# Decay sums of an SSD mixer read back from a DRAM scratch, and dt computed from the residual stream

## The chip, the cores and the metric

One core of a Trainium2 chip. Times are device microseconds (us) of one launch. The engines are named as in the profile: PE (matmuls) with PEld (its weight loads), DVE (VectorE), ACT (ScalarE), POOL (GpSimd), SP (which issues most DMAs).

## The reference, cut to what matters

Two layers (DEPTH 2), each a half-step SwiGLU FFN, a mixer and another half-step FFN, over 256 prompt tokens and 8 x 4 sample tokens (T = 288 columns), D_MODEL 1024. The part that is changed is the decay of the mixer's SSD branch, 16 heads, chunks of 128 tokens:

```
h  = rmsnorm(x, mix_norm)
dt = softplus((h @ w_in)[dt columns, 16] + dt_bias)
la = dt * (-exp(a_log))
acum = cumsum(la)                                  # per head, within a chunk
decay = exp(where(causal, acum[t] - acum[s], -inf))
y_diag = einsum(cb * decay, x * dt)                # cb = C.B per group
to_end = exp(acum[-1] - acum); from_start = exp(acum)
```

## The kernel before, in words

The activations lie transposed: feature on the partitions, 288 tokens along the free axis, `x` as 8 tiles of 128 features. Every large product runs in three float32r parts (`mm3`, line 271): weight high x activation high, high x low, low x high. The weights arrive as 439 slabs of 8 tiles of 128 x 128 (`Stream`): SP loads a slab (`raw`, 4 buffers), ACT makes the high part (`whi`, line 137, 4 buffers), DVE the low part (`wlo`, line 145, 3 buffers), PE runs 24 matmuls on it (`ps`). The high part is asked for three slabs ahead, the low part two.

The order of all work is written by hand. At the start of each slab `tick` loads, splits, and calls `step`, which runs every small generator of the mixer (`dt_work`, `conv`, `heads4`, ...) up to its next `yield`; a delay given to `W.start` counts such steps. Each engine executes what it was given in that order. Matmul results go to 7 rotating PSUM banks (tag `b`).

What the change touches:

- Lines 603 to 606 split the 1024 x 16 dt weights into a high and a low part side by side (`wds`, 48 columns); line 1242 on runs 16 float32r matmuls on them with the high and low part of the normed input (`ps_dt`).
- `dt_work` (line 663) forms dt and its cumulative sums `nac` (16 heads x 288) and splits them once more into `nst`. With masked copies (`sbd`) and products with ones (`ps_ee`, `ps_rb`, `ps_eb`) it spreads the sample group's sums over the partitions, into `Ee`, `Eb` and `Ms`.
- `heads4(g)` (line 859) handles four heads of the prompt group. `rows` multiplies `nst` with one broadcast column of `sel2`, so that a head's row of 256 sums stands on all 128 partitions in PSUM (`ps_row`); `decay` reads it from there into `E` on ACT; `E` is multiplied by the masked C.B on DVE and enters `outputs` on PE (`ps_y`). `E` has two buffers. The four calls start at steps 7, 11, 15 and 19 (line 1196).

Of the kernel before, what the change touches and what calls it, by code (L numbers as in the profile page):

```python
# [38 lines left out]
H = 16  # L39
# [146 lines left out]
def trunk_kernel(ctx, tc, wpack, xT, memT, vecs, consts, wdt, wpool, hpool, hconv, h0T, kT, vC,  # L186
# [46 lines left out]
    def tt(out, a, b, op, eng=None):  # L233
        (eng or V).tensor_tensor(out=out, in0=a, in1=b, op=op)  # L234
# [13 lines left out]
    def act(out, a, func, **kw):  # L248
        A.activation(out=out, in_=a, func=func, **kw)  # L249

    W = Stream(nc, rawp, splp, wpack)

    vec = cp.tile([P, V_TOT], F32, name="vec")
# [13 lines left out]
    def hi_of(hi, src, scale=None):  # L267
        if scale is None:
            act(hi, src, AF.Copy)
        else:  # L270
            act(hi, src, AF.Copy, scale=scale)

    def lo_of(lo, src, hi, scale=None):
        if scale is None:
            tt(lo, src, hi.bitcast(F32), ALU.subtract)
        else:
            stt(lo, src, scale, hi.bitcast(F32), ALU.mult, ALU.subtract)
# [172 lines left out]
    rv = cp.tile([P, 2], F32, name="rv")  # L450
    sel2 = cp.tile([P, H], F32R, name="sel2")
    nst = cp.tile([P, TP], F32R, name="nst")
    G.memset(nst.bitcast(F32), 0.0)
    sel4 = cp.tile([P, 4], F32R, name="sel4")
# [14 lines left out]
    def mem_norm():  # L469
        for c in range(KC):  # L470
            src = chunk(mem, c)[:, :NM]
            if c == 0:
                act(macc, src, AF.Square)
            else:
                sq = tmp("sqr", NM)
                act(sq, src, AF.Square)
                tt(macc, macc, sq, ALU.add)
            if c % 4 == 3:
                yield
        yield  # L480
        r = rstd_cols([macc], (0, P), D, "mem")
        V.tensor_copy(out=rv, in_=r)
        yield
        ps = bank("ps_rm")
        for j in range(2):
            mm(ps[:, j * P:(j + 1) * P], rv[:, j:j + 1].to_broadcast([P, P]), ident)
        act(Rm, ps[:, :NM], AF.Copy)
        act(sel4, ident.rearrange("p (a b) -> p a b", a=4)[:, :, 0], AF.Copy)
        act(sel2, con[:, K_SEL:K_SEL + H], AF.Copy)

# [106 lines left out]
    def mixer(i, cur, nxt):  # L597
# [4 lines left out]
        nc.sync.dma_start(out=wd, in_=wdt[i])  # L602
        wds = sp.tile([P, KC, 48], F32R, tag="wds", name="wds")
        G.memset(wds[:, :, H:2 * H].bitcast(F32), 0.0)
        hi_of(wds[:, :, 0:H], wd)
        lo_of(wds[:, :, 2 * H:], wd, wds[:, :, 0:H])
        wp_ = sp.tile([P, 4, P], F32, tag="wp", name="wp")
# [32 lines left out]

        npar = sp.tile([32 + H, T], F32, tag="nac", name="nac")
        nac, par = npar[:H], npar[32:, :P]
        nact = sp.tile([P, 3, H], F32, tag="nact", name="nact")
# [19 lines left out]
        def dt_work(ps_dt):  # L663
            dtr = tmp("dtr", T, 48)
            tt(dtr, ps_dt[:48, :T], cur.R[:48], ALU.mult)
            S = [P, 3, H]
# [5 lines left out]
            for j, (a, n) in enumerate(CH):  # L672
                mm(pt[:n, j * H:(j + 1) * H], dtr[:, a:a + n], con[:48, K_SEL:K_SEL + H])
            bias = vec[:, i * V_N + V_DT:i * V_N + V_DT + H]
# [31 lines left out]
            mm(pw[:TS, 2 * H:3 * H], sst, la[:TS, 2, :])  # L706
            act(nst[0:H, :], ph[:H, :TP], AF.Copy)
            V.tensor_copy(out=nac, in_=ph[:H, :T])
            tt(nst[32:32 + H, :], nac[:, :TP], nst[0:H, :].bitcast(F32), ALU.subtract)
            act(wt[:, 0, :], pw[:, 3 * H:4 * H], AF.Exp, scale=-1.0)  # L710
            act(wt[:, 1, :], pw[:, H:2 * H], AF.Exp, scale=-1.0)
            act(wt[:TS, 2, :], pw[:TS, 2 * H:3 * H], AF.Exp, scale=-1.0)
            ts(b01, pw[:, 0:H], -1.0, ALU.mult)
            ex = tmp("dex", TS, H)
            act(ex, nac[:, TP:T], AF.Exp, scale=-1.0)
            act(par, con[:H, K_PAR:K_PAR + P], AF.Copy)
            sb = wide("sbd", P, TP)
            hh = H // 2
            for j in range(2):
                o = sb[96 * j:96 * j + H, :]  # L720
                tt(o.rearrange("p (h t) -> p h t", h=hh), nac[:, TP:T].unsqueeze(1).to_broadcast([H, hh, TS]),
                   ident[:H, hh * j:hh * j + hh].unsqueeze(2).to_broadcast([H, hh, TS]), ALU.mult)
            tt(sb[32:32 + H, :].rearrange("p (a t) -> p a t", a=8), ex.unsqueeze(1).to_broadcast([H, 8, TS]),
               con[:H, K_PM:K_PM + 8].unsqueeze(2).to_broadcast([H, 8, TS]), ALU.mult)
            tt(sb[64:64 + H, :P].rearrange("p (b h) -> p b h", b=DB), seg(ex)[:, :, 3:4].to_broadcast([H, DB, H]),
               ident[:H, :H].unsqueeze(1).to_broadcast([H, DB, H]), ALU.mult)
            yield
            pt, pd = bank("ps_nact"), bank("ps_ee")
            for j, (a, n) in enumerate(CH):
                PE.transpose(pt[:n, j * H:(j + 1) * H], nac[:, a:a + n], ident[:H, :H])  # L730
            mm(pd[:, :P], ones[64:64 + H, :], sb[64:64 + H, :P])
            yield
            ts(nact[:, 0:2].rearrange("p a h -> p (a h)"), pt[:, :2 * H], -1.0, ALU.mult)
            V.tensor_copy(out=nact[:TS, 2], in_=pt[:TS, 2 * H:3 * H])
            V.tensor_copy(out=Ee.rearrange("p b h -> p (b h)"), in_=pd[:, :P])
            pr = [bank("ps_rb") for j in range(2)]
            pe = bank("ps_eb")
            mm(pr[0][:, :TP], ones[:H, :], sb[:H, :])
            mm(pe[:, :TP], par, sb[32:32 + H, :])
            mm(pr[1][:, :TP], ones[96:96 + H, :], sb[96:96 + H, :])  # L740
            yield
            V.tensor_copy(out=Eb.rearrange("p a t -> p (a t)"), in_=pe[:, :256])
            for j in range(2):
                tt(Ms[:, hh * j:hh * j + hh], nact[:TS, 2, hh * j:hh * j + hh].unsqueeze(2).to_broadcast([TS, hh, TS]),
                   pr[j][:TS, :TP].rearrange("p (h t) -> p h t", h=hh), ALU.subtract)
            ts(Ms, Ms, 0.0, ALU.min)
# [112 lines left out]
        def heads4(g):  # L859
# [3 lines left out]
            def rows(pi):  # L863
                prow = bank("ps_row")
                for j in range(2):
                    h = 4 * g + 2 * pi + j
                    mm(prow[:, j * TP:(j + 1) * TP], sel2[:, h:h + 1].to_broadcast([P, P]), nst)
                return prow

            def decay(pi, prow):  # L870

                E = ep.tile([P, 2, 3 * P], F32, tag="E", name="E")
                for j in range(2):
                    h = 4 * g + 2 * pi + j
                    for t_ in range(2):
                        act(E[:, j, TP * t_:TP * t_ + P], prow[:, j * TP + P * t_:j * TP + P * t_ + P], AF.Relu,
                            bias=nact[:, t_, h:h + 1])
                    act(E[:, j, P:TP], prow[:, j * TP + P:(j + 1) * TP], AF.Exp, scale=-1.0, bias=b01[:, h:h + 1])
                e = E.rearrange("p j (a t) -> p j a t", a=3)[:, :, 0:3:2, :]
                act(e, e, AF.Exp, scale=-1.0)  # L880
                return E

# [15 lines left out]
            def finish(pi, py):  # L898
# [5 lines left out]
                nc.sync.dma_start(out=o_ssm_p[i, p], in_=st)  # L904

            px = bank("ps_x")
            for t_ in range(2):
                for pi in range(2):
                    k = t_ * TP + pi * P
                    PE.transpose(px[:, k:k + P], chunk(xsu, 2 * g + pi)[:, t_ * P:(t_ + 1) * P], ident)  # L910
            r0 = rows(0)
            yield
# [5 lines left out]
               wt[:, 0:2, hs].unsqueeze(3).to_broadcast([P, 2, 4, 64]), ALU.mult)  # L918
            E0 = decay(0, r0)
            r1 = rows(1)  # L920
            yield
            E1 = decay(1, r1)
            yield
            for E in (E0, E1):
                tt(E, E, cbm[:, g, :].unsqueeze(1).to_broadcast([P, 2, 3 * P]), ALU.mult)
            yield
            ys = outputs((E0, E1))
            yield
# [254 lines left out]
        for kind, cs, tiles, cuts in mixer_groups():  # L1183
# [10 lines left out]
            if kind == "u" and c == 0:  # L1194
                items["xss"] = W.start(xss_work(), 3)
                items["pairs"] = [W.start(sample_diag(), 6)] + [W.start(heads4(g), 7 + 4 * g) for g in range(4)]
                items["ss"] = [W.start(sample_state(b), 14 + 2 * b) for b in range(DB)]
                items["yo"] = W.start(sample_y(), 33)
                items["gn"] = W.start(group_norm(), 36)
# [38 lines left out]
            elif kind == "q":  # L1238
# [4 lines left out]
                for k in range(KC):  # L1243
                    mm(ps_dt[:48, :T], wds[:, k, :], chunk(xh, k), k == 0, False)
                    mm(ps_dt[:48, :T], wds[:, k, :], chunk(xl, k), False, k == KC - 1)
                items["dt"] = W.start(dt_work(ps_dt))
# [137 lines left out]
```

## Time and profile before

| | us |
|---|---|
| median of 3 runs (lowest, highest) | 1548.44 (1547.94, 1549.15) |
| the profiled execution, whole | 1547.92 |
| its span, first to last instruction | 1546.1 |
| PE busy | 1530.3 |
| DVE busy | 1064.0 |
| ACT busy | 824.3 |
| POOL busy | 192.1 |

Busy times are unions of an engine's instructions within the span; a matmul's end is modelled, and matmuls overlap in the pipeline, so what one costs is the distance from its start to the next start, not its own duration. The engines overlap each other. One profiled execution was read; it lies 0.5 us below the median.

### The profile page before, as it was taken

The page shows a single profiled execution, that of the slowest core. Times are in us where ns is not written, and L with a number is a line of the kernel's source. Part 1 is how long each engine was busy: PE and PEld are TensorE (multiplying, and loading weights), DVE is VectorE, ACT ScalarE, POOL GpSimd, SP SyncE. Part 2 cuts the span into 40 slices and gives each one's busy share as a digit, 9 for nine tenths or more (in the row PEclk, how much of TensorE's full clock was granted, in tenths as well). Part 3 has the DMA queues.
Part 4 walks back from the last instruction along what each step waited for, and adds up shares of the span by engine and source line. Part 5 has one row for each costly group of instructions (what it writes and reads, how often), then busy time and mean ns, then how long its engine had stood idle before and what let it go on. Part 6 is the DMA issues. An engine that isn't in the chain of part 4 may idle for free.

```text
span 1546.1 us, 29133 instructions
## 1 busy us (share of the span) xinstructions
PE 1530.3 (99%) x11740; PEld 1491.3 (96%) x11740; DVE 1064.0 (69%) x1674; ACT 824.3 (53%) x1268; POOL 192.1 (12%) x284
## 2 busy tenths in 40 slices
PE   9999999999999999999999999999999999999998
PEld 7999999899989999999999999999998999999997
DVE  7766655899678877665566665579978787766643
ACT  7544444566864645444445444457587464544442
POOL 0100001245003111000010000024600120100001
PEclk9999999999999999999999999999999999999999
DMA  8655455566466445455545544556655745555552
GB/s 294 220 167 166 168 165 171 188 231 230 147 210 221 164 157 173 164 167 169 166 152 173 168 164 164 171 190 206 230 172 193 249 152 162 166 165 167 166 169 73
DMA packets 80711, 278.00 MB, mean 180 GB/s; under 512 B 9024, under 2 KB 13248, under 8 KB 80576
## 3 DMA queue, kind: packets, MB, share of 16 engines
q1 hardware_dynamic: 79872, 275.28, 53.5%
q8 instruction: 92, 1.51, 0.4%
q10 hardware_dynamic: 704, 0.86, 0.2%
q14 instruction: 43, 0.35, 0.1%
HBM read 262.39 MB, written 13.71 MB: 179 GB/s over the span
## 4 chain that ended last, share of the span: by engine, by line
PE 93%; DVE 4%; ACT 1%; issue 1%; DMA 1%; ACTq 0%; DVEq 0%
PE ps L246 65%; PE pd L246 18%; PE ps_v L246 1%; PE ps_y L246 1%; PE ps_k L246 1%; DVE wlo L145 1%; DVE cacc L243 1%; PE ps_up L246 1%; PE ps_yo L246 1%; PE ps_sp L246 0%; PE ps_pv L246 0%; ACT whi L137 0%; PE ps_cb L246 0%; DVE cbuf L234 0%; DMA cb<-kT 0%
## 5 line engine op out<-in xcount | busy, mean ns | idle before, releaser
L145 DVE TENSOR_TENSOR wlo<-raw,whi 128x1024 fp32r<-128x1024 f32 (+1 forms) x441 | 552.3, 1254 | 255.8 <-ACT hidh L249 102.5
L137 ACT ACTIVATE whi<-raw 128x1024 fp32r<-128x1024 f32 (+1 forms) x441 | 464.0, 1054 | 328.1 <-PE ps L246 161.1
L246 PE MATMUL ps<-n1h,whi 128*128 128x288 f32 x896 | 270.6, 302 | 4.1 <-DVE gate L234 2.1
L246 PE MATMUL ps<-n1l,whi 128*128 128x288 f32 x896 | 264.4, 295 | 0.0
L246 PE MATMUL ps<-n1h,wlo 128*128 128x288 f32 x896 | 263.7, 294 | 0.0
L246 PE MATMUL ps<-n2h,whi 128*128 128x288 f32 x704 | 208.9, 297 | 0.0
L246 PE MATMUL ps<-n0h,whi 128*128 128x288 f32 x704 | 208.8, 297 | 0.0
L246 PE MATMUL pd<-hidh,whi 128*128 128x288 f32 x704 | 208.4, 296 | 0.0
L246 PE MATMUL ps<-n0l,whi 128*128 128x288 f32 x704 | 207.8, 295 | 0.0
L246 PE MATMUL pd<-hidl,whi 128*128 128x288 f32 x704 | 207.8, 295 | 0.0
L246 PE MATMUL ps<-n2l,whi 128*128 128x288 f32 x704 | 207.8, 295 | 0.0
L246 PE MATMUL ps<-n0h,wlo 128*128 128x288 f32 x704 | 207.1, 294 | 0.0
L246 PE MATMUL pd<-hidh,wlo 128*128 128x288 f32 x704 | 207.1, 294 | 0.0
L246 PE MATMUL ps<-n2h,wlo 128*128 128x288 f32 x704 | 207.1, 294 | 0.0
L246 PEld LDWEIGHTS ps<-n1h,whi 128*128 128x128 f32 x896 | 168.1, 188 | 8.5 <-DVE gate L234 2.5
L246 PEld LDWEIGHTS ps<-n1l,whi 128*128 128x128 f32 x896 | 168.4, 188 | 0.6
L246 PEld LDWEIGHTS ps<-n1h,wlo 128*128 128x128 f32 x896 | 168.6, 188 | 0.0
L234 POOL TENSOR_TENSOR acc<-acc,sqr 128x288 f32<-128x288 f32 x42 | 48.6, 1158 | 801.3 <-ACT sqr L249 800.0
L246 PEld LDWEIGHTS ps<-n2h,wlo 128*128 128x128 f32 x704 | 132.7, 188 | 0.0
L246 PEld LDWEIGHTS pd<-hidh,wlo 128*128 128x128 f32 x704 | 132.7, 188 | 0.0
L246 PEld LDWEIGHTS ps<-n0h,wlo 128*128 128x128 f32 x704 | 132.7, 188 | 0.0
L246 PEld LDWEIGHTS ps<-n0l,whi 128*128 128x128 f32 x704 | 132.2, 188 | 0.1
(314 smaller groups left out, 2720.2 us busy)
## 6 DMA issues: line engine op xcount, KB each, us to landing
raw<-wpack SPq DMA_DIRECT2D x439, 512.0 KB, 3.3
cb<-kT SPq DMA_DIRECT2D x16, 512.0 KB, 5.5
cb<-vC SPq DMA_DIRECT2D x16, 512.0 KB, 4.9
hb<-h0T SPq DMA_DIRECT2D x16, 512.0 KB, 5.5
o_ssm_s<-hb SPq DMA_DIRECT2D x16, 512.0 KB, 5.0
x<-xT SPq DMA_DIRECT2D x4, 288.0 KB, 6.1
o_mk<-ksb SPq DMA_DIRECT2D x2, 512.0 KB, 6.1
o_mv<-vsb SPq DMA_DIRECT2D x2, 512.0 KB, 5.4
```

What stands on the lines that cost most here:

```text
L137: nc.scalar.activation(out=hi[:, a], in_=self.loaded[self.n_hi][:, a], func=AF.Copy)
L145: nc.vector.tensor_tensor(out=lo[:, a], in0=raw[:, a], in1=self.his[n][:, a].bitcast(F32), op=ALU.subtract)
L234: (eng or V).tensor_tensor(out=out, in0=a, in1=b, op=op)
L243: V.scalar_tensor_tensor(out=out, in0=a, scalar=s, in1=b, op0=op0, op1=op1)
L246: PE.matmul(out, lhsT=lhsT, rhs=rhs, start=start, stop=stop)
```

## The change

dt comes from the unsplit residual `x` in plain float32: the norm's gain is multiplied into the 1024 x 16 weights, which stand in 32 columns (16 of them zero), and the eight products go to four column groups of the PE array in turn; their four partial sums are added by the transposing matmul with `sel4h`. The sums `nac` and the exponentials of the sample group are written to a DRAM scratch `sums`, the last ones of each sample to `lasts`; `Ms`, `Eb` and `Ee` are read back from there by SP with stride 0 over the partitions. `rows` becomes two DMAs issued by POOL that read a pair of heads' sums straight into `E`; the ACT instructions of `decay` work there in place. `heads4` has one more step, and its four calls start at steps 6, 11, 16 and 21.

```diff
+    sums = nc.dram_tensor("sums", (L, H, T + TS), F32).ap()
+    lasts = nc.dram_tensor("lasts", (L, DB, H), F32).ap()
...
-        wds = sp.tile([P, KC, 48], F32R, tag="wds", name="wds")
-        G.memset(wds[:, :, H:2 * H].bitcast(F32), 0.0)
-        hi_of(wds[:, :, 0:H], wd)
-        lo_of(wds[:, :, 2 * H:], wd, wds[:, :, 0:H])
+        wds = sp.tile([P, KC, 2 * H], F32, tag="wds", name="wds")
+        G.memset(wds[:, :, H:], 0.0)
+        gain = vec[:, i * V_N + V_MIX:i * V_N + V_MIX + KC]
+        tt(wds[:, :, 0:H], wd, gain.unsqueeze(2).to_broadcast([P, KC, H]), ALU.mult)
...
-            dtr = tmp("dtr", T, 48)
-            tt(dtr, ps_dt[:48, :T], cur.R[:48], ALU.mult)
+            dtr = tmp("dtr")
+            tt(dtr, ps_dt[:, :T], cur.R, ALU.mult)
...
-                mm(pt[:n, j * H:(j + 1) * H], dtr[:, a:a + n], con[:48, K_SEL:K_SEL + H])
+                mm(pt[:n, j * H:(j + 1) * H], dtr[:, a:a + n], sel4h)
...
-            act(nst[0:H, :], ph[:H, :TP], AF.Copy)
-            V.tensor_copy(out=nac, in_=ph[:H, :T])
-            tt(nst[32:32 + H, :], nac[:, :TP], nst[0:H, :].bitcast(F32), ALU.subtract)
+            V.tensor_copy(out=nac[:, :T], in_=ph[:H, :T])
+            ex = nac[:, T:]
+            act(ex, ph[:H, TP:T], AF.Exp, scale=-1.0)
...
-            for j in range(2):
-                o = sb[96 * j:96 * j + H, :]
-                tt(o.rearrange("p (h t) -> p h t", h=hh), nac[:, TP:T].unsqueeze(1).to_broadcast([H, hh, TS]),
-                   ident[:H, hh * j:hh * j + hh].unsqueeze(2).to_broadcast([H, hh, TS]), ALU.mult)
...
...
-            mm(pd[:, :P], ones[64:64 + H, :], sb[64:64 + H, :P])
+            nc.sync.dma_start(out=sums[i], in_=nac)
+            nc.sync.dma_start(out=lasts[i].rearrange("b h -> h b").unsqueeze(2), in_=seg(ex)[:, :, 3:4])
             yield
...
-            mm(pr[0][:, :TP], ones[:H, :], sb[:H, :])
-            mm(pe[:, :TP], par, sb[32:32 + H, :])
-            mm(pr[1][:, :TP], ones[96:96 + H, :], sb[96:96 + H, :])
-            yield
-            V.tensor_copy(out=Eb.rearrange("p a t -> p (a t)"), in_=pe[:, :256])
+            nc.sync.dma_start(out=Ms, in_=sums[i, :, TP:T].unsqueeze(0).to_broadcast([TS, H, TS]))
...
+                nc.sync.dma_start(out=Eb[64 * j:64 * j + 64], in_=src.to_broadcast([64, 8, TS]))
+            nc.sync.dma_start(out=Ee, in_=lasts[i].unsqueeze(0).to_broadcast([P, DB, H]))
+            yield
+            yield
+            tt(Ms, nact[:TS, 2].unsqueeze(2).to_broadcast([TS, H, TS]), Ms, ALU.subtract)
...
             def rows(pi):
-                prow = bank("ps_row")
-                for j in range(2):
-                    h = 4 * g + 2 * pi + j
-                    mm(prow[:, j * TP:(j + 1) * TP], sel2[:, h:h + 1].to_broadcast([P, P]), nst)
-                return prow
+                E = ep.tile([P, 2, 3 * P], F32, tag="E", name="E")
+                src = sums[i, 4 * g + 2 * pi:4 * g + 2 * pi + 2].unsqueeze(0)
+                G.dma_start(out=E[:, :, 0:TP], in_=src[:, :, 0:TP].to_broadcast([P, 2, TP]))
+                G.dma_start(out=E[:, :, TP:], in_=src[:, :, P:TP].to_broadcast([P, 2, P]))
+                return E
...
+            Es = [rows(pi) for pi in range(2)]
+            yield
             px = bank("ps_x")
...
-                items["pairs"] = [W.start(sample_diag(), 6)] + [W.start(heads4(g), 7 + 4 * g) for g in range(4)]
+                items["pairs"] = [W.start(sample_diag(), 6)] + [W.start(heads4(g), 6 + 5 * g) for g in range(4)]
...
-                    mm(ps_dt[:48, :T], wds[:, k, :], chunk(xh, k), k == 0, False)
-                    mm(ps_dt[:48, :T], wds[:, k, :], chunk(xl, k), False, k == KC - 1)
+                    mm(ps_dt[32 * (k % 4):32 * (k % 4) + 32, :T], wds[:, k, :], x[:, k, :], k < 4, k >= 4)
```

## Rows read from the trace of the kernel before

**Rows 1.** The page's part 1: busy time, share of the span, instructions

```profile
PE 1530.3 (99%) x11740; PEld 1491.3 (96%) x11740; DVE 1064.0 (69%) x1674; ACT 824.3 (53%) x1268; POOL 192.1 (12%) x284
```

**Rows 2.** PE's waits over the span: us in total, times, longest

```profile
PE ps L246 <- DVE gate L234: 2.1, 2, 1.0
PE ps L246 <- DVE cbuf L234: 1.7, 2, 0.9
```

**Rows 3.** The chain in order of time: start us, us, what

```profile
279.22 2.10 PE ps_dt L246 x16
384.39 0.49 PE ps_pool L246 x2
395.09 0.23 PE ps_row L246 x2
504.40 0.62 PE ps_gn L246 x8
```

**Rows 4.** PE by timeline: start us, us, what, [idle before <-releaser]

```profile
302.20 0.46 PE L246 MATMUL ps_ee<-sbd,con 16*128 16x128 f32 x2
302.59 0.40 PE L246 MATMUL ps<-n1h,whi 128*128 128x288 f32 x1
305.98 0.48 PE L246 MATMUL ps_rb<-sbd,con 16*128 16x256 f32 x1
307.55 0.37 PE L246 MATMUL ps<-n1h,whi 128*128 128x288 f32 x1 [0.86 <-DVE cbuf L234]
```

**Rows 5.** The tile ps_row: PE's idle time before its matmuls, times

```profile
  PE ps_row L246: 1.3, 4
```

**Rows 6.** DVE by timeline, dt_work and the first heads4

```profile
299.27 0.42 DVE L234 TENSOR_TENSOR nst<-nac,nst 16x256 fp32r<-16x256 f32 x1
300.50 0.83 DVE L234 TENSOR_TENSOR sbd<-nac,con 16x256 f32<-16x256 f32 x2
301.34 0.71 DVE L234 TENSOR_TENSOR sbd<-dex,con 16x256 f32<-16x256 f32 x2
312.00 0.42 DVE L742 COPY Eb<-ps_eb 128x256 f32<-128x256 f32 x1
381.35 0.51 DVE L243 SCALAR_TENSOR_TENSOR ypl<-ps_pool,vec,yph 128x288 fp32r<-128x288 f32 x1
```

**Rows 7.** Busy time by stretch: PE, PEld, DVE, ACT, POOL, then PE clock, DMA share, GB/s

```profile
310.00:338.00 28.00, 28.00 (x226) 26.53 (x225) 27.12 (x53) 21.16 (x35) 13.60 (x32) 1.00 0.66 234
338.00:382.00 44.00, 43.73 (x454) 41.95 (x454) 41.62 (x83) 27.20 (x52) 26.73 (x44) 1.00 0.60 215
400.00:420.00 20.00, 20.00 (x155) 18.48 (x154) 11.90 (x24) 19.88 (x41) 0.00 (x0) 1.00 0.49 157
420.00:460.00 40.00, 38.94 (x303) 35.05 (x303) 32.49 (x53) 28.46 (x55) 0.00 (x0) 1.00 0.59 190
```

**Rows 8.** POOL by timeline, its last instruction before 400 us

```profile
376.84 0.28 POOL L1001 COPY po<-ub 128x120 f32<-128x120 f32 x1
```

**Rows 9.** ACT by timeline, the first heads4 and later

```profile
376.24 0.62 ACT L249 ACTIVATE E<-ps_row,nact 128x128 f32<-128x128 f32 x2 [0.49 <-PE ps_row L246]
379.70 0.52 ACT L249 ACTIVATE yph<-ps_pool,vec 128x288 fp32r<-128x288 f32 x1
444.55 0.58 ACT L249 ACTIVATE pp<-ps_ptp 128x512 f32<-128x512 f32 x1
448.47 0.72 ACT L249 ACTIVATE bm<-Bst,con 96x512 fp32r<-96x512 f32 x1
```

**Rows 10.** DMA issues by line: issuer, count, KB each, median us to landing

```profile
cb<-kT SPq DMA_DIRECT2D x16, 512.0 KB, 5.5
o_ssm_p<-st SPq DMA_DIRECT2D x16, 64.0 KB, 3.0
```

**Rows 11.** The page's part 3, ACT's DMA queue: packets, MB, share of 16 engines

```profile
q10 hardware_dynamic: 704, 0.86, 0.2%
```

**Rows 12.** What SP's queue waited for: us in total, times, longest

```profile
SPq L128 <- DVE wlo L145: 1187.8, 413, 7.2
```

More of the change, by code (lines that the diff above doesn't have):

```diff
@@ L450, in trunk_kernel @@
     rv = cp.tile([P, 2], F32, name="rv")
-    sel2 = cp.tile([P, H], F32R, name="sel2")
-    nst = cp.tile([P, TP], F32R, name="nst")
-    G.memset(nst.bitcast(F32), 0.0)
+    sel4h = cp.tile([P, H], F32, name="sel4h")
+    G.memset(sel4h, 0.0)
     sel4 = cp.tile([P, 4], F32R, name="sel4")
@@ L488, in mem_norm @@
         act(sel4, ident.rearrange("p (a b) -> p a b", a=4)[:, :, 0], AF.Copy)
-        act(sel2, con[:, K_SEL:K_SEL + H], AF.Copy)
+        for j in range(4):
+            act(sel4h[32 * j:32 * j + H], ident[32 * j:32 * j + H, 32 * j:32 * j + H], AF.Copy)
     def load_x():
@@ L639, in conv @@
                 nc.sync.dma_start(out=o_conv[i], in_=co)
-        npar = sp.tile([32 + H, T], F32, tag="nac", name="nac")
-        nac, par = npar[:H], npar[32:, :P]
+        nac = sp.tile([H, T + TS], F32, tag="nac", name="nac")
         nact = sp.tile([P, 3, H], F32, tag="nact", name="nact")
@@ L713, in dt_work @@
             ts(b01, pw[:, 0:H], -1.0, ALU.mult)
[L714 to L718, printed above, removed]
-            for j in range(2):
-                o = sb[96 * j:96 * j + H, :]
-                tt(o.rearrange("p (h t) -> p h t", h=hh), nac[:, TP:T].unsqueeze(1).to_broadcast([H, hh, TS]),
-                   ident[:H, hh * j:hh * j + hh].unsqueeze(2).to_broadcast([H, hh, TS]), ALU.mult)
[L723 to L726, printed above, removed]
             yield
-            pt, pd = bank("ps_nact"), bank("ps_ee")
+            pt = bank("ps_nact")
             for j, (a, n) in enumerate(CH):
                 PE.transpose(pt[:n, j * H:(j + 1) * H], nac[:, a:a + n], ident[:H, :H])
-            mm(pd[:, :P], ones[64:64 + H, :], sb[64:64 + H, :P])
+            nc.sync.dma_start(out=sums[i], in_=nac)
+            nc.sync.dma_start(out=lasts[i].rearrange("b h -> h b").unsqueeze(2), in_=seg(ex)[:, :, 3:4])
             yield
@@ L734, in dt_work @@
             V.tensor_copy(out=nact[:TS, 2], in_=pt[:TS, 2 * H:3 * H])
-            V.tensor_copy(out=Ee.rearrange("p b h -> p (b h)"), in_=pd[:, :P])
-            pr = [bank("ps_rb") for j in range(2)]
-            pe = bank("ps_eb")
-            mm(pr[0][:, :TP], ones[:H, :], sb[:H, :])
-            mm(pe[:, :TP], par, sb[32:32 + H, :])
-            mm(pr[1][:, :TP], ones[96:96 + H, :], sb[96:96 + H, :])
+            nc.sync.dma_start(out=Ms, in_=sums[i, :, TP:T].unsqueeze(0).to_broadcast([TS, H, TS]))
+            for j in range(2):
+                src = sums[i, :, T:].rearrange("(a j) t -> j a t", j=2)[j:j + 1]
+                nc.sync.dma_start(out=Eb[64 * j:64 * j + 64], in_=src.to_broadcast([64, 8, TS]))
+            nc.sync.dma_start(out=Ee, in_=lasts[i].unsqueeze(0).to_broadcast([P, DB, H]))
             yield
-            V.tensor_copy(out=Eb.rearrange("p a t -> p (a t)"), in_=pe[:, :256])
-            for j in range(2):
-                tt(Ms[:, hh * j:hh * j + hh], nact[:TS, 2, hh * j:hh * j + hh].unsqueeze(2).to_broadcast([TS, hh, TS]),
-                   pr[j][:TS, :TP].rearrange("p (h t) -> p h t", h=hh), ALU.subtract)
+            yield
+            tt(Ms, nact[:TS, 2].unsqueeze(2).to_broadcast([TS, H, TS]), Ms, ALU.subtract)
             ts(Ms, Ms, 0.0, ALU.min)
@@ L863, in rows, with decay @@
             def rows(pi):
-                prow = bank("ps_row")
-                for j in range(2):
-                    h = 4 * g + 2 * pi + j
-                    mm(prow[:, j * TP:(j + 1) * TP], sel2[:, h:h + 1].to_broadcast([P, P]), nst)
-                return prow
-            def decay(pi, prow):
-                E = ep.tile([P, 2, 3 * P], F32, tag="E", name="E")
+                E = ep.tile([P, 2, 3 * P], F32, tag="E", name="E")
+                src = sums[i, 4 * g + 2 * pi:4 * g + 2 * pi + 2].unsqueeze(0)
+                G.dma_start(out=E[:, :, 0:TP], in_=src[:, :, 0:TP].to_broadcast([P, 2, TP]))
+                G.dma_start(out=E[:, :, TP:], in_=src[:, :, P:TP].to_broadcast([P, 2, P]))
+                return E
+            def decay(pi, E):
                 for j in range(2):
@@ L875, in decay @@
                     for t_ in range(2):
-                        act(E[:, j, TP * t_:TP * t_ + P], prow[:, j * TP + P * t_:j * TP + P * t_ + P], AF.Relu,
-                            bias=nact[:, t_, h:h + 1])
-                    act(E[:, j, P:TP], prow[:, j * TP + P:(j + 1) * TP], AF.Exp, scale=-1.0, bias=b01[:, h:h + 1])
+                        e = E[:, j, TP * t_:TP * t_ + P]
+                        act(e, e, AF.Relu, bias=nact[:, t_, h:h + 1])
+                    act(E[:, j, P:TP], E[:, j, P:TP], AF.Exp, scale=-1.0, bias=b01[:, h:h + 1])
                 e = E.rearrange("p j (a t) -> p j a t", a=3)[:, :, 0:3:2, :]
                 act(e, e, AF.Exp, scale=-1.0)
-                return E
             def outputs(Es):
@@ L910, in heads4 @@
                     PE.transpose(px[:, k:k + P], chunk(xsu, 2 * g + pi)[:, t_ * P:(t_ + 1) * P], ident)
-            r0 = rows(0)
             yield
@@ L918, in heads4 @@
                wt[:, 0:2, hs].unsqueeze(3).to_broadcast([P, 2, 4, 64]), ALU.mult)
-            E0 = decay(0, r0)
-            r1 = rows(1)
+            decay(0, Es[0])
             yield
-            E1 = decay(1, r1)
+            decay(1, Es[1])
             yield
-            for E in (E0, E1):
+            for E in Es:
                 tt(E, E, cbm[:, g, :].unsqueeze(1).to_broadcast([P, 2, 3 * P]), ALU.mult)
             yield
-            ys = outputs((E0, E1))
+            ys = outputs(Es)
             yield
```

## The prediction, made before the changed kernel was run

> **What bounds the kernel now.** I read the busy times first, then PE's waits, then the mixer by stretches, then the order of single instructions. PE is busy for 1530.3 us, 99% of the span [rows 1]. Over the whole span PE's recorded waits for another engine's result are a few single microseconds; of those that lie in the mixer, 2.1 us are for `gate` and 1.7 us for `cbuf`, each twice, so once in each layer [rows 2]. So an instruction taken from PE is worth its full time, unless another engine cannot follow. There the reader should look at DVE: it is busy for 27.12 of 28 us from 310 to 338 and for 41.62 of 44 us from 338 to 382; ACT takes over for a while, 19.88 of 20 us from 400 to 420, and DMA stands at 0.49 to 0.66 [rows 7]. PE's granted clock is 1.00 in all these stretches, the 2.4 GHz level; I expect no change of it, since PE stays busy.
>
> **The change, part by part.** All figures are for one layer and are doubled at the end; the second layer repeats the pattern of the first. The code is the same in both.
>
> *dt on PE.* The 16 matmuls leave; they take 2.10 us [rows 3]. In their place come 8 float32 products of 128 x 32 by 288, on four column groups. The trace has exactly this shape: `ps_gn`, four products (8 instructions, since a float32 product is two) on four column groups, 0.62 us [rows 3]. Two such rounds are 1.24 us, so 0.86 us are saved. If the groups did not overlap, the nearest row is `ps_pool`, one full-width float32 product over 288 columns, 0.49 us [rows 3]: eight are 3.92 us, a loss of 1.82 us. I take `ps_gn`, the same shape and the same alternation. The multiplication of the result by R covers more partitions at the same width, which I cost at nothing; the preparation of `wds` loses an ACT copy and keeps one DVE instruction; both happen ahead of the stage.
>
> *The sample group's spreading products.* `ps_ee` goes: 302.59 - 302.20 = 0.39 us. `ps_rb` and `ps_eb` go: from 305.98 to 307.55 less the 0.86 us of waiting, 0.71 us [rows 4]. The transposes into `ps_nact` stay.
>
> *The rows of heads.* Sixteen matmuls in eight pairs, a pair 0.23 us [rows 3]: 1.84 us.
>
> *PE's sum.* 0.86 + 0.39 + 0.71 + 1.84 = 3.80 us, 7.6 us in two layers.
>
> *The wait for `cbuf`.* It stands right behind `ps_rb` and `ps_eb` [rows 4]: all banks are taken, three of them by these products, and DVE is late. Ahead of this `cbuf` DVE loses the `nst` subtraction and the four `sbd` copies, 0.42 + 0.83 + 0.71 = 1.96 us [rows 6], more than the 0.86 us of the wait, and the three banks are not asked for. So the wait goes, 1.7 us in two layers. What is late next is DVE itself, a little later in the stage. There it loses 0.42 us more (`Eb`), and a copy of `Ee`; `Ms` is one subtraction in place of two halves. Together about 2.4 us or more, against 2.8 us (0.86 + 0.39 + 0.71 + 0.86) by which PE comes earlier: DVE keeps pace within half a microsecond.
>
> *The scratch writes and SP's reads.* `sums` and `lasts` are written one step after `nac`, and read one step later; `Ms` is used two steps behind that. A step is a slab and what is put between, about 3.4 us (305.98 - 302.59) [rows 4]. A 64 KB store lands in 3.0 us [rows 10], so SP waits some tenths for the scratch, or up to 3 us if stores to it are slower. Behind it in SP's queue are the slab loads, and SP idles for most of the span, waiting for buffers that `wlo` frees, 1187.8 us in 413 waits [rows 12]; I cost it at nothing. For `Ms`, 6.8 us stand against 5.5 us for a 512 KB load [rows 10] with far more bytes; many small pieces could make it slower. If it is late, DVE waits at the subtraction with `cacc`, `cbuf` and `wlo` behind it; I bound this from 0 to 2 us and take 0.
>
> *The E transfers.* A pair of heads needs 256 pieces of 1 KB and 256 of 512 bytes. No row has a DMA issued by POOL; the nearest queue of small packets is ACT's, 704 packets for 0.2% of 16 engines' span, 1546.1 x 16 x 0.002 / 704 = 70 ns at most each [rows 11]. Eight pairs are 4096 packets, 287 us or 18 us on 16 engines, over some 80 us: the DMA share rises by at most 0.22, to about 0.8 [rows 7]. The slab loads have several slabs of lead; cost 0. For the landing I take 3.0 us (64 KB) to 5.5 us (512 KB) [rows 10] from the issue, plus POOL's time to issue, for which only its own instructions can stand: from 0.28 us, a copy [rows 8], to the mean over all of them, 192.1 / 284 = 0.68 us [rows 1]. With two DMAs for a pair at the dearer end that is 4.4 to 6.9 us.
>
> *Where E is waited for.* POOL executes in order. For the first group the transfers stand behind `pool_mix`, whose last instruction ends at 376.84 + 0.28 = 377.1 us [rows 8], while ACT took up the first row at 376.24 [rows 9]. So E is there at 381.5 to 384.0 us, 5 to 8 us after ACT could use it. Behind `decay` on ACT stand `yph`, at 379.70 [rows 9], and the high parts; DVE's `ypl`, at 381.35 [rows 6], waits for `yph` and delays the emptying of banks. The two row banks are free now and high parts are made three slabs ahead, so I cost the first group at 0, with 2 us a layer as the other end. For the later groups E's buffers come free with the previous group's `ps_y`, and ACT gets to them two steps later, 6.8 us against 4.4 to 6.9: cost 0; beyond it see the third rival. ACT then reads SBUF in place of PSUM: 512 wide that is 0.72 against 0.58 us [rows 9]; 48 instructions at up to 0.14 us are 6.7 us in some 80 us. ACT has the room from 420 to 460 (28.46 of 40 us) and not from 400 to 420 [rows 7]; the new starts (steps 11, 16, 21) also move it; 0.
>
> **The sum.** 7.6 + 1.7 = 9.3 us. The profiled execution took 1547.92 us, which makes 1538.6; the median is 0.5 us above it, so **1539.1 us**. Unknown on the good side are the waits for `gate`, 2.1 us [rows 2], and 1.3 us of idle time ahead of `ps_row` [rows 5]: 3.4 us, down to 1535.7. On the other side stands the first group, 4 us: 1543.1.
>
> **The rivals.**
>
> *First: part of the gain is lost at the first group.* POOL's backlog speaks for it, the free banks against. At twice the bound, 4 us a layer, 1547. I centre it on 1544.
>
> *Second: DVE cannot follow.* It is at 95% from 310 to 382 [rows 7]. If all that PE saves before 382 (0.86 + 0.39 + 0.71 + 0.86, and two row pairs, 0.46: 3.28 us) comes back as waits for banks, 6.6 us are lost: 1545.7, no measurable change. Against it: DVE loses nearly the same there.
>
> *Third: slower, E is late in every group.* ACT's wait holds back the high parts. The lead that can be used up is one step before ACT gets there and two slabs of low parts, 3 x 3.4 = 10.2 us from the issue; each further microsecond is paid by PE in four groups and two layers. From 11.8 us on (8 x 1.6 = 12.4 = 9.3 + 3.1) the kernel is slower; at 13 us it takes 1539.1 + 8 x 2.8 = 1561.5. For it: nothing shows how POOL issues, and ACT is full from 400 to 420. Against: 512 KB land in 5.5 us.
>
> The Trainium skill, page "SBUF — State Buffer", section "SBUF: two separate sides", speaks against the change: a DMA issued by GpSimd has its descriptors written by GpSimd itself, which is shut out while VectorE runs an operation in a two-port mode. Its part "A bandwidth-pool intuition that's wrong (but worth ruling out)" gives 620 ns alone and 3100 ns beside such a copy; an estimate from this page would be 2.5 us for each of a group's four DMAs, 10 us on top of 5.5, and 1581 us by the third rival's rule. No run here shows it yet.
>
> *Fourth: the column groups do not overlap.* dt then costs 2 x 2.68 us more: 1544.5. `ps_gn` speaks against it.
>
> **Chances.** About 0.2% (3.1 us) is what a measurement of this kernel tells from no change: 1545.3 to 1551.5. Forecast 0.60; first rival 0.14, faster still; second 0.13, the same; third 0.10, slower; fourth 0.03, faster. So faster 0.77, same 0.13, slower 0.10. The forecast's own range is 1535.7 to 1543.1; with most of the first, the fourth and part of the second it reaches to 1546.
>
> **What would show it.** `ps_dt` at 1.1 to 1.4 us, no `ps_row`, `ps_rb`, `ps_eb` and `ps_ee`; no wait for `cbuf` near 307; PE busy some 7 to 8 us less; the median landing of E under 7 us; ACT's wait for E in the first group alone. Wrong would be PE's waits for `cbuf`, `z` or `wlo` of over 1 us a group, or `ps_dt` near 4 us.

## The result and the profile after

The changed kernel takes 1560.09 us (median of 4; 1558.60 to 1560.39), the kernel before 1548.19 on the same chip: a ratio of 1.0074 [1.0059, 1.0089], 11.9 us slower. The forecast was 1539.1 us, faster, and the range ended at 1546. The profiled execution took 1560.36 us, 12.4 more than that of before.

Busy time of the changed kernel, from part 1 of its page; it answers to [rows 1]:

```profile
PE 1530.1 (98%) x11692; PEld 1486.7 (95%) x11692; DVE 1062.7 (68%) x1658; ACT 831.4 (53%) x1269; POOL 210.7 (14%) x316
```

PE's waits of the changed kernel (total us, times, longest); they answer to [rows 2]:

```profile
PE ps_s L246 <- DMA cb<-kT: 12.2, 5, 4.5
PE ps_up L246 <- DVE part L234: 2.6, 2, 1.3
PE ps_pv L246 <- ACT pp L249: 2.3, 2, 1.2
...
PE ps_y L246 <- ACT pr L249: 1.3, 2, 0.7
```

The waits for `gate` and `cbuf` are gone, 3.8 us. Four others have come or grown, 18.4 us, of which `kT` had 0.6 before. None of them is for the data of the change: the largest is for `kT`, the keys of the sample group's memory attention, an old load. PE's own timeline (start us, us, [idle before <-releaser]):

```profile
279.44 1.18 PE L246 MATMUL ps_dt<-x,wds 128*32 128x288 f32 x16
...
323.60 1.08 PE L246 MATMUL ps_s<-cb,qm 128*32 128x256 f32 x8 [4.46 <-DMA cb<-kT]
326.13 1.08 PE L246 MATMUL ps_s<-cb,qm 128*32 128x256 f32 x8 [1.44 <-DMA cb<-kT]
```

The DMA issues of the changed kernel (count, KB each, median us to landing); `kT` answers to [rows 10]:

```profile
cb<-kT SPq DMA_DIRECT2D x16, 512.0 KB, 6.7
E<-sums POOLq DMA_DIRECT2D x16, 256.0 KB, 4.8
E<-sums POOLq DMA_DIRECT2D x16, 128.0 KB, 5.3
...
sums<-nac SPq DMA_DIRECT2D x2, 20.0 KB, 6.6
lasts<-nac SPq DMA_DIRECT2D x2, 0.5 KB, 8.9
```

The E transfers land as forecast. The smallest DMA of the program, `lasts`, 128 stores of 4 bytes, takes longest.

To see where the time went I cut each mixer at starts of PE instructions, the same in every kernel: first `ps_dt`; the second round of score products `ps_s`, which is the one that needs the late `kT`; `ps_cb`; `ps_cbs`; and, behind a stretch that hardly changes (`ps_cbs` to `ps_yd`, 30.6 to 31.0 us in all of these), `ps_yd` to `ps_gn`, which holds all of `heads4`. In us, first layer / second layer, worked out from the traces:

| kernel | dt to `ps_s` | `ps_s` to `ps_cb` | `ps_cb` to `ps_cbs` | `ps_yd` to `ps_gn` | median |
|---|---|---|---|---|---|
| before | 41.5 / 41.4 | 1.9 / 2.6 | 15.6 / 15.6 | 135.8 / 135.3 | 1548.2 |
| after | 38.1 / 38.1 | 9.6 / 9.2 | 17.7 / 16.5 | 136.0 / 135.9 | 1560.1 |
| e14 (before + `lasts`) | 41.5 / 41.5 | 6.0 / 6.2 | 18.0 / 16.7 | 135.6 / 135.6 | 1559.7 |
| e12 (`lasts` in 32 B) | 38.1 / 38.1 | 4.0 / 3.6 | 15.6 / 15.6 | 136.8 / 136.6 | 1548.0 |
| e18 (before, later starts) | 41.5 / 41.5 | 1.9 / 2.7 | 15.6 / 15.6 | 139.2 / 138.7 | 1555.2 |
| e17 (all mended) | 38.1 / 38.1 | 1.9 / 1.9 | 15.6 / 15.6 | 131.8 / 131.8 | 1535.0 |

Three things are to be explained in after: 14.3 us lost at `ps_s`, 3.1 us right behind it, and a last stage that should have become shorter by the eight row pairs, 1.84 us a layer, and did not. Only the first stage shows the gain, 3.3 us a layer.

### The profile page after: what moved, and what is told of

It is laid out like the page before. It is cut to its first block, busy times and chain, and to the rows that moved or that the text cites. A ratio compares the mean times of both kernels' runs of the same rounds, so it can differ in the third digit from the quotient of the medians.

```text
span 1558.6 us, 29115 instructions
## 1 busy us (share of the span) xinstructions
PE 1530.1 (98%) x11692; PEld 1486.7 (95%) x11692; DVE 1062.7 (68%) x1658; ACT 831.4 (53%) x1269; POOL 210.7 (14%) x316
## 3 DMA queue, kind: packets, MB, share of 16 engines
q0 software_dynamic: 2048, 6.29, 1.7%
## 5 line engine op out<-in xcount | busy, mean ns | idle before, releaser
L246 PEld LDWEIGHTS ps<-n2l,whi 128*128 128x128 f32 x704 | 132.1, 188 | 0.1
```

The costliest lines, as they stand in the source:

```text
L246: PE.matmul(out, lhsT=lhsT, rhs=rhs, start=start, stop=stop)
```

## The experiments

The expectations call the theories by letters, as each says; in words, the main ones are: SP's queue stands still for the scratch (A); the E transfers crowd the loads (B); the 4-byte store `lasts` jams the DMA engines (D); the moved starts of `heads4` put its exponentials in ACT's way (F). The kernel before was run again beside each experiment, with medians of 1548.2 to 1549.2 us; so the ratio, not the bare median, compares two experiments.

**e1_defer: is it SP's order?** The scratch is read four steps later, so that SP does not stand at `Ms` ahead of the loads.

```diff
+            for _ in range(4):
+                yield
             nc.sync.dma_start(out=Ms, in_=sums[i, :, TP:T]...)
```

> The changed kernel, with the reads of the scratch into Ms, Eb and Ee issued four steps later, behind the last of the loads of kT. Theory A (the reads stand in SP's queue, wait there for the scratch write to land and hold up the last kT loads, for which PE waits at ps_s): the wait of 12.2 us and the slower clock behind it, some 3 us, go; 1542 to 1546 us. Theory C (kT had no lead before either, and PE now merely arrives earlier, by some 3 us a layer): 2 to 3 us of wait a layer stay; 1546 to 1549. Theory B (the transfers into E and the later heads4 are what costs): no change, 1558 to 1561.

Measured: 1555.9 us, 1.0046 [1.0031, 1.0061]. SP no longer stands at `Ms`, but most of PE's wait for `kT` stays, as the waits and the DMA issues of e1 show:

```profile
PE ps_s L246 <- DMA cb<-kT: 8.4, 4, 3.4
```
```profile
cb<-kT SPq DMA_DIRECT2D x16, 512.0 KB, 7.3
```

The loads were issued sooner and took longer. SP's order is a part, 3.8 of 12.2 us; the main part is a slow transfer.

**e2_kt_early: is it only that `kT` has no lead?** The second round of scores starts two slabs sooner and its products stand where they were, so `kT` is loaded ahead of the jam.

```diff
+            for _ in range(2 * q):
+                yield
...
-                items["sc"] = [W.start(scores(q), 2 + 7 * q) for q in range(2)]
+                items["sc"] = [W.start(scores(q), 2 + 5 * q) for q in range(2)]
```

> The changed kernel, with the second four kT loads started two steps earlier and their products left at the same step; all of them then stand ahead of the scratch reads in SP's queue. A and C: the wait at ps_s falls under 1 us a layer in this run, since neither the reads nor a missing lead is left; 1541 to 1545 us, and under C lower than the run that only defers the reads. B: 1558 to 1561.

Measured: 1559.81 us, 1.0078 [1.0061, 1.0094]. The wait for `kT` is gone and others have come; PE's waits of e2:

```profile
PE ps L246 <- DVE wlo L145: 4.2, 3, 2.7
PE ps_pv L246 <- ACT pp L249: 3.4, 2, 1.8
PE ps_sp L246 <- DMA kp<-o_mk: 3.3, 2, 1.7
PE ps_av L246 <- POOL cbuf L626: 2.7, 2, 1.5
```

A slab's low part is late now: the weight loads are caught in the same stretch. The slab load issued at 307.37 us took 8.7 us to land, where the one at 308.56 in before took 3.5, and the next one was issued behind `Ms` in SP's queue as well. Whatever is in flight there is late, so the cause isn't in the `kT` loads.

**e3_rows_pe: is it the E transfers?** The rows of heads come from PE again, with the old starts; the sample group keeps the scratch.

```diff
-                E = ep.tile([P, 2, 3 * P], F32, tag="E", name="E")
...
+                prow = bank("ps_row")
+                for j in range(2):
+                    mm(prow[:, j * TP:(j + 1) * TP], sel2[:, h:h + 1].to_broadcast([P, P]), nst)
```

> The changed kernel, with the heads' rows multiplied on PE again (nst, sel2, ps_row, starts 7, 11, 15, 19) and nothing of E from the scratch; the sample group's Ms, Eb and Ee still come from it. A: the wait for kT stays near 12 us; PE has 3.7 us more, the stalls of the later stretch are back as before; 1558 to 1562 us. B: what the E transfers cost goes; 1542 to 1548.

Measured: 1559.98 us, 1.0073 [1.0058, 1.0088], with no E transfer in the program. The wait of e3 for `kT`:

```profile
PE ps_s L246 <- DMA cb<-kT: 14.4, 5, 6.2
```

So B is not the cause of that wait.

**e4_e_only: the other half.** The sample group's values are spread by PE again, `lasts` and the reads of `Ms`, `Eb`, `Ee` leave; `sums` is still written and E still read from it.

```diff
             nc.sync.dma_start(out=sums[i], in_=nac)
-            nc.sync.dma_start(out=lasts[i].rearrange("b h -> h b").unsqueeze(2), in_=seg(ex)[:, :, 3:4])
```

> The changed kernel, with Ms, Eb and Ee spread by products on PE again; only the E transfers read the scratch, and SP has one small scratch write and no read. A: the wait for kT falls to 0 to 3 us a layer; PE has 2.2 us more in all; 1543 to 1550 us. B: 1558 to 1562.

Measured: 1555.31 us, 1.0038 [1.0023, 1.0053]. In the profiled execution the wait for `kT` is back at the 0.6 us of before and `sums` lands in 4.2 us. That execution took 1551.91 us, 3.4 below the median, so its waits show less than the median lost. But the kernel is still slower than before, by stalls far behind this place; PE's waits of e4:

```profile
PE ps_pv L246 <- ACT pp L249: 4.2, 2, 2.4
PE ps_up L246 <- DVE part L234: 2.6, 2, 1.3
...
PE ps_y L246 <- ACT pr L249: 1.3, 2, 0.7
...
PE ps_s L246 <- DMA cb<-kT: 0.6, 1, 0.6
```

This points to two causes: one in the small scratch traffic and one that comes with `heads4`. The next experiments take each of them alone.

**e14_before_lasts: the 4-byte store alone.** The kernel before, with one DMA for each layer that nobody reads: the same 128 values of 4 bytes, 0.5 KB, from SBUF to DRAM.

```diff
+    lasts = nc.dram_tensor("lasts", (L, DB, H), F32).ap()
...
+            nc.sync.dma_start(out=lasts[i].rearrange("b h -> h b").unsqueeze(2), in_=seg(ex)[:, :, 3:4])
```

> The kernel before, with nothing changed but one more DMA in dt_work: the 128 four-byte pieces of the last exponentials are written to a scratch that nobody reads. D: the DMA rate falls under 100 GB/s for some 7 us behind it, the second kT loads land 4 to 6 us later than before, PE waits 3 to 6 us a layer at ps_s and runs at a lower clock behind it; 1553 to 1562 us. A: a store of 0.5 KB that nobody waits for costs nothing; 1548 to 1550.

Measured: 1559.74 us, 1.0074 [1.0059, 1.0089]: two DMAs of half a kilobyte cost as much as the whole change lost. Nothing waits for them, so all of it is what they do to others. The DMA issues of e14:

```profile
cb<-kT SPq DMA_DIRECT2D x16, 512.0 KB, 6.5
...
lasts<-dex SPq DMA_DIRECT2D x2, 0.5 KB, 9.2
```

The stretches tell how. The columns are busy time of PE, PEld, DVE, ACT, POOL, then PE's clock, DMA share and GB/s; the stretch is 311 to 315, first before, then e14, then after:

```profile
311.00:315.00 4.00, 4.00 (x32) 4.00 (x32) 3.89 (x8) 3.92 (x5) 1.45 (x4) 1.00 0.79 305
```
```profile
311.00:315.00 4.00, 4.00 (x33) 4.00 (x32) 3.90 (x10) 3.74 (x5) 1.54 (x4) 1.00 0.77 48
```
```profile
311.00:315.00 4.00, 4.00 (x32) 4.00 (x31) 1.85 (x4) 2.79 (x3) 1.54 (x4) 1.00 0.42 40
```

The DMA engines of before and e14 are busy for nearly the same share, and e14 moves less than a sixth of the bytes. In the trace's packet records of e14, packets of 4096 bytes that start from 311 to 312 take 1304 ns on average, against 159 in before; the rate is 30 to 60 GB/s from 311 to 317, where before has 230 to 400 up to 316.

The table shows how this and the gain of the first stage meet. From `ps_dt` to `ps_cb` e14 takes 47.5 / 47.7 us and after 47.7 / 47.3, against 43.4 / 44.0 in before. So the late loads set the time at which `ps_cb` can start, and the 3.3 us a layer by which PE comes earlier in after are waited away: after loses 14.3 us at `ps_s`, and e14, which has no gain to lose, 7.7.

**e12_lasts32: the same values in larger pieces.** In the changed kernel `lasts` is stored as 16 rows of 32 bytes, from a compact tile, and `Ee` is read in that order; all else stays.

```diff
-            nc.sync.dma_start(out=lasts[i].rearrange("b h -> h b").unsqueeze(2), in_=seg(ex)[:, :, 3:4])
+            act(exl, ph[:H, TP:T].rearrange("p (b t) -> p b t", b=DB)[:, :, 3], AF.Exp, scale=-1.0)
...
+            nc.sync.dma_start(out=lasts[i], in_=exl)
```

> The changed kernel, with the last exponentials written to the scratch as 16 rows of 8 contiguous values (32 bytes), from a small compact tile, in place of 128 pieces of 4 bytes; Ee is read in that order. Theory D (the 128 four-byte stores stop the DMA engines for some 7 us, and the kT loads behind them land late): the stretch of under 100 GB/s behind the write goes, sums lands in about 4 us as in the run with E alone, the wait at ps_s falls from 12.2 us to 2 to 6 us in all; 1545 to 1551 us. Theory A (the order in SP's queue and the reads): the wait stays over 8 us; 1555 to 1560.

Measured: 1547.97 us, 0.9998 [0.9989, 1.0008]: 12.1 us less than after. The DMA issues of e12:

```profile
sums<-nac SPq DMA_DIRECT2D x2, 20.0 KB, 4.1
lasts<-exl SPq DMA_DIRECT2D x2, 0.5 KB, 3.9
```

`lasts` lands in 3.9 us in place of 8.9, and `sums`, which is issued ahead of it, in 4.1 in place of 6.6. With e14 this settles D: the store is sufficient by itself, and cutting it into fewer pieces takes the loss away. Size and number of the pieces, their strided source and their order in DRAM changed together, so which of these matters is open. PE still waits 3.4 us for `kT`, which e1's deferral takes away (e15).

**e18_before_starts: the second cause.** The kernel before, with nothing but later starts for `heads4`: 7, 12, 17, 22 for 7, 11, 15, 19.

```diff
-                items["pairs"] = [W.start(sample_diag(), 6)] + [W.start(heads4(g), 7 + 4 * g) for g in range(4)]
+                items["pairs"] = [W.start(sample_diag(), 6)] + [W.start(heads4(g), 7 + 5 * g) for g in range(4)]
```

> The kernel before, with only the starts of the four heads4 calls moved from 7, 11, 15, 19 to 7, 12, 17, 22, so that decay comes at the steps that it has in the changed kernel; rows stay on PE. Theory F (the moved decay of the second group meets the silu of z, the gates and their table loads on ACT, which is full there): PE's waits of 1 to 1.5 us each at ps_pv and ps_up, and 0.7 at ps_y, appear as in the changed kernel, and the stretch from ps_yd to ps_gn grows from 135.8 and 135.3 to 137 to 139 us; 1550 to 1554 us. Rival (they come with E from SBUF and its transfers): the stretch stays within 0.5 us; 1548 to 1549.

Measured: 1555.16 us, 1.0043 [1.0026, 1.0060], about 6 us more than before. PE waits in e18 at the same places as in after, although no row comes from DRAM:

```profile
PE ps_up L246 <- DVE part L234: 2.6, 2, 1.3
...
PE ps_pv L246 <- ACT pp L249: 1.5, 2, 0.8
...
PE ps_y L246 <- ACT pr L249: 1.3, 2, 0.7
```

For the wait at `ps_pv` ACT's timelines show why, first before, then after:

```profile
408.28 0.46 ACT L249 ACTIVATE pr<-ps_sp,mx 128x256 f32<-128x256 f32 x1
...
408.85 1.28 ACT L249 ACT_TABLE_LOAD   x1
410.15 0.96 ACT L249 ACTIVATE gate<-gate,vec 128x288 f32<-128x288 f32 x2
411.01 1.04 ACT L137 ACTIVATE whi<-raw 128x1024 fp32r<-128x1024 f32 x1
411.96 0.58 ACT L249 ACTIVATE pp<-ps_ptp 128x512 f32<-128x512 f32 x1
```

```profile
413.77 0.47 ACT L249 ACTIVATE pr<-ps_sp,mx 128x256 f32<-128x256 f32 x1
...
414.22 0.69 ACT L249 ACTIVATE E<-E,nact 128x128 f32<-128x128 f32 x2
...
416.62 1.28 ACT L249 ACT_TABLE_LOAD   x1
417.91 0.96 ACT L249 ACTIVATE gate<-gate,vec 128x288 f32<-128x288 f32 x2
418.78 1.04 ACT L137 ACTIVATE whi<-raw 128x1024 fp32r<-128x1024 f32 x1
419.73 0.57 ACT L249 ACTIVATE pp<-ps_ptp 128x512 f32<-128x512 f32 x1
```

The second group's decay, 2.4 us from 414.22 to 416.62, now stands between the softmax `pr` and the `gate` with its table load, and `pp`, for which PE's `ps_pv` waits, comes after all of it. In before the stretch from 408.28 (`pr`) to 411.96 (`pp`) is 3.7 us; in after, from 413.77 to 419.73, it is 6.0. ACT was full there before the change [rows 7]. The waits for `part` and `pr`, 3.9 of the 6.2 us in after, come with the new starts as well, since e18 has them; how is not shown. In after DVE makes `part` at 427.99 behind `hb`, for which it had waited 5.77 us on PE's `ps_yo`, so that one is not ACT's lateness alone.

**e5_dt_only: dt alone, on the kernel before.**

```diff
-                    mm(ps_dt[:48, :T], wds[:, k, :], chunk(xh, k), k == 0, False)
-                    mm(ps_dt[:48, :T], wds[:, k, :], chunk(xl, k), False, k == KC - 1)
+                    mm(ps_dt[32 * (k % 4):32 * (k % 4) + 32, :T], wds[:, k, :], x[:, k, :], k < 4, k >= 4)
```

> The kernel before, with only dt taken from the residual stream on four column groups. PE's ps_dt takes 1.1 us in place of 2.1; if that gain holds, 1546 to 1547 us. If PE's earlier arrival is taken back by the kT loads (theory C), PE waits about 1 us more at ps_s in each layer and the time stays at 1548 to 1549.

Measured: 1546.28 us, 0.9987 [0.9977, 0.9996], some 2.1 us less than before. `ps_dt` takes 1.1 us from its start to the next start, and the first stage falls from 41.5 to 40.4. This part of the gain holds.

**e15_all: both causes mended.** e12 and e1 together, a third E buffer (with temporaries of 320 columns in place of 384) so that starts can stand at 6, 10, 14, 18, and the second pair's rows asked for one step later.

```diff
-    ep = ctx.enter_context(tc.tile_pool(name="ep", bufs=2))
+    ep = ctx.enter_context(tc.tile_pool(name="ep", bufs=3))
...
-            Es = [rows(pi) for pi in range(2)]
+            Es = [rows(0)]
...
+            Es.append(rows(1))
...
-                items["pairs"] = [W.start(sample_diag(), 6)] + [W.start(heads4(g), 6 + 5 * g) for g in range(4)]
+                items["pairs"] = [W.start(sample_diag(), 6)] + [W.start(heads4(g), 6 + 4 * g) for g in range(4)]
```

> The changed kernel with three edits: the last exponentials as 32-byte rows, the scratch reads four steps later, and the E transfers with a third buffer, the heads4 calls at steps 6, 10, 14, 18, so that decay comes at the steps that it had in the kernel before and the first pair's E of a group is asked for without waiting for the group before it. D: the first part as in the run with the 32-byte rows, with the wait at ps_s under 2 us a layer. For the later stretch (from ps_yd to ps_gn, 135.8 us before and 136.0 after), if the stalls there come from E's lateness and the moved decay: 133.5 to 134.5 us; if from something else: over 135.5. In all 1538 to 1545 us.

Measured: 1542.04 us, 0.9959 [0.9944, 0.9974]. The stalls at `kT`, `pp`, `part` and `pr` are gone, but `ps_yd` to `ps_gn` did not fall to what I expected: 136.7 us. What came in their place is the prediction's first rival. POOL's, ACT's, DVE's and PE's timelines of e15, in one view:

```profile
373.86 0.87 POOL L857 DMA_DIRECT2D E<-sums  x1
...
378.72 0.40 ACT L249 ACTIVATE E<-E,nact 128x128 f32<-128x128 f32 x1 [6.03 <-DMA E<-sums]
...
384.82 0.52 DVE L243 SCALAR_TENSOR_TENSOR ypl<-ps_pool,vec,yph 128x288 fp32r<-128x288 f32 x1 [4.67 <-ACT yph L249]
...
387.20 1.10 PE L246 MATMUL ps_sp<-kp,q 128*128 128x256 f32 x4 [3.15 <-DVE ym L1092]
```

POOL reaches E's issue only behind its copies for `pool_mix`; ACT waits for E, DVE for ACT, PE for DVE: 3.1 us in the first layer. In the second PE waits 2.5 us for the load of `kp`.

**e16_e0_early and e17_kv_early.** e16 asks for the first group's E four steps sooner; e17 also loads `kp` two slabs sooner.

```diff
+            for _ in range(1 if g else 5):
+                yield
...
-                items["pairs"] = [W.start(sample_diag(), 6)] + [W.start(heads4(g), 6 + 4 * g) for g in range(4)]
+                items["pairs"] = [W.start(sample_diag(), 6)] + [W.start(heads4(g), 6 + 4 * g if g else 2) for g in range(4)]
...
-                items["kv"] = W.start(load_prompt_kv(), 28)
+                items["kv"] = W.start(load_prompt_kv(), 26)
```

> The run with all three edits, and the first group's E transfers asked for four steps earlier, ahead of the last pool_mix adds on POOL. If the 3.1 us of PE in the first layer at ps_sp come down the chain POOL's backlog, E, ACT's yph, DVE's ypl, a bank (the first rival of the prediction): ACT's wait for the first E (6.0 and 1.8 us) and DVE's wait for yph (4.7 us) fall under 0.5 us, and PE's wait with them, unless the kp load, for which PE waits 2.5 us in the second layer, is late there as well; 1537 to 1541 us. If ACT is late for another reason: no change, 1541 to 1543.

> The run before it in this list, and the load of the prompt's keys (kp) asked for two steps earlier. If kp is late only because PE now comes to ps_sp earlier and its load is slowed by the E transfers: PE's wait for kp, up to 2.5 us a layer, goes; 1535.5 to 1539 us. If the wait is the bank behind ps_avt: no change against the run before it.

Measured: e16 1539.98 us, 0.9942 [0.9927, 0.9957]; the wait for `ym` is gone, that for `kp` stays (3.7 us in two layers). e17 1534.99 us, 0.9912 [0.9897, 0.9926]: 14.2 us less than before, and faster than both kernels. Part 1 of e17's page:

```profile
PE 1522.3 (99%) x11692; PEld 1483.5 (97%) x11692; DVE 1060.8 (69%) x1658; ACT 821.0 (54%) x1263; POOL 213.8 (14%) x316
```

The profiled span of e17 is 1533.0 us, 13.1 less than that of before. PE is busy 8.0 us less than in [rows 1]; the other 5.1 us are idle time of PE, and 4.4 of them are waits of before that are gone: 2.1 for `gate`, 1.7 for `cbuf` [rows 2] and 0.6 for `kT`.

## Why the prediction was wrong

*PE's own terms: right.* dt took 1.11 us, not 1.24, and the column groups overlapped, so the fourth rival did not occur. `ps_ee`, `ps_rb`, `ps_eb` and `ps_row` left and the wait for `cbuf` went; dt to `ps_s` fell by 3.3 us, against 2.8 counted for dt, the sample group and `cbuf`. DVE kept pace there, so the second rival did not occur. PE's busy time did not fall in after, although these instructions are gone. Of the granted clock the prediction says "I expect no change of it, since PE stays busy", and that was wrong: PE waited for `kT`, and its clock fell to 0.50 (last section). In e12, where it stayed at 1.00 there, PE is busy for 1524.5 us, and in e17 8.0 us less than in before, against 7.6 counted.

*The scratch writes, "I cost it at nothing": the step that failed.* I priced `lasts` by its bytes, from a 64 KB store, and asked only how long SP would wait for it. Its price was on everybody else's transfers: 11.4 us in e14. The bound "up to 3 us if stores to it are slower" was of the right kind for SP's wait, which was 5.1 us at the longest, and missed the loads in flight; e1 shows what SP's place in the queue was worth, 3.8 of the 12.2 us at `ps_s`. Of what stands behind the scratch in SP's queue I named only the slab loads, with SP idle for most of the span [rows 12]. The `kT` loads stand there too, and the waits of before already had PE 0.6 us late on them, a row that I did not use:

```profile
PE ps_s L246 <- DMA cb<-kT: 0.6, 1, 0.6
```

The cost followed there. The Trainium skill, page "DMA: Bandwidth & Descriptors", section "Specifications", says that a transfer below 512 bytes is done as a read-modify-write and misses line rate; that would have been a rule to weigh against the change. The trace agrees that the pieces of 4 bytes are slow (8.9 us to landing) and doesn't show it for pieces of 32 (3.9 us); a read-modify-write itself no run here shows. By that rule alone the store is slow, and not yet the loads behind it, which is where the time went.

*The starts of `heads4`, "the new starts (steps 11, 16, 21) also move it; 0": the second step that failed.* I looked at ACT's share from 420 to 460 and not at what stood in the very place to which the second group moved. e18 prices the starts alone at some 6 us. In after the last stage's sum closes: 135.8 less 1.84 for the rows, less half of the 2.1 for `gate`, plus half of 6.2 for `part`, `pp` and `pr`, is 136.0, which is what it took.

*The E transfers: right in the main.* They landed in 4.8 and 5.3 us, against 4.4 to 6.9; POOL spent 0.72 us on an issue, just above the 0.28 to 0.68. The third rival did not occur; in its working 8 x 1.6 is 12.8 and not 12.4, on which nothing else hangs. No run shows the 2.5 us that the prediction estimated from the Trainium skill, page "SBUF — State Buffer", section "SBUF: two separate sides", nor tests it: beside E's issues DVE ran only TENSOR_TENSOR and SCALAR_TENSOR_TENSOR instructions in after, and no copy. The DMA share was over-counted a little: 2048 packets and 1.7% of 16 engines' span, some 13 us a layer in place of 18. ACT waited for E in the first group, as foreseen, and for some 3 of its 9.2 us in the fourth, which was not; PE has no wait that comes from it in after. ACT's pair of 128-wide instructions (`E<-E,nact`) took 0.69 us from SBUF, against 0.62 from PSUM [rows 9]: little lost there.

*The first group, costed at 0 "with 2 us a layer as the other end": right in after, and wrong as soon as the rest was mended.* In after PE was late enough for E; in e15 it cost 3.1 us in one layer, by the chain that the first rival names.

*The lower end of the range: a row misread.* The 1.3 us of [rows 5], put on the good side as idle time ahead of `ps_row`, are not PE's. They are time in which ACT, which reads `ps_row`, waited for PE, as the same view of before says under "who waited for it":

```profile
  ACT E L249: 1.3, 4
```

So the good side had 2.1 us and not 3.4, which makes 1537.0 and not 1535.7. This changes nothing in why the change was slower.

*Slower was foreseen only by E being late* (chance 0.10). What made it slower was in no rival.

*What stays open.* The stages account for 11.5 of the 12.5 us between the spans; of the last one 0.4 lies ahead of the first `ps_dt` and 0.6 behind the last `ps_gn`, and its cause was not followed. How the new starts bring about the waits for `part` and `pr` is not shown. Why 128 pieces of 4 bytes hold up 16 DMA engines, and from which number or size on, was not tried.

## What to carry to other kernels

Price a DMA by its pieces and by what is in flight behind it, not only by its bytes or by who waits for it: here a store of 128 pieces of 4 bytes that nobody read cost more than the change was worth. Before calling a load's lead ample, look for the one load of the stretch that PE already waits for. When steps are moved on a schedule written by hand, read the timeline of the place that they are moved to; and after mending one stall, expect the next, which was hidden behind it.

## What the runs showed of the hardware

- 128 stores of 4 bytes in one DMA: 4096-byte packets behind them took 1.3 us on average in the worst microsecond of e14's first layer and 1.8 us in that of after, in place of 0.16, and the rate stayed under 70 GB/s for some 6 us. With 16 stores of 32 bytes the rate in e12 was 290 to 410 GB/s from 306 to 311. It fell to 120 to 180 from 311 to 314, while the reads of `Ms`, `Eb` and `Ee` ran; e15, with these reads four steps later, has no such dip there.
- The late loads cost more than the waits for them, through PE's clock. In after PE was idle for 4.46 and 1.44 us; its granted clock, 0.63 on average from 320 to 326, was at the 1.2 GHz level (0.50) from 326 to 330 and at the 2.4 GHz level again from 334 on:

```profile
320.00:326.00 6.00, 1.08 (x8) 0.20 (x8) 5.86 (x13) 4.83 (x9) 2.11 (x5) 0.63 0.98 372
326.00:330.00 4.00, 3.87 (x18) 2.88 (x19) 3.93 (x8) 2.94 (x6) 2.69 (x6) 0.50 0.49 177
330.00:334.00 4.00, 4.00 (x24) 3.95 (x24) 3.07 (x10) 1.11 (x3) 0.46 (x5) 0.77 0.37 131
334.00:345.00 11.00, 11.00 (x85) 10.73 (x84) 10.70 (x18) 8.36 (x14) 6.29 (x13) 1.00 0.53 192
```

  The stage behind the wait took 2.2 us more in the first layer and 0.9 in the second. In e14, after waits of 1.38 and 1.90 us in the first layer, the clock fell as well. From `ps_s` to `ps_cbs` e14 loses 11.2 us in the two layers: 6.1 are longer waits (6.7 against 0.6), and the other 5.1 are the same instructions taking longer, 3.5 of it behind the waits. In e12, with a single wait of 1.9 us at most in a layer, the clock stayed at 1.00 there and the stage took 15.6 us as before.
